# Hybrid trunk on one core: the last output group's weights loaded and split beside the first two output groups

## The chip, the cores and the metric

The kernel runs on one core of a Trainium2 chip. The metric is device time in microseconds (us) of one execution. A core has TensorE (PE, the matmuls), VectorE (DVE), ScalarE (ACT), GpSimd (POOL) and SyncE (SP, which here only issues DMA transfers). Each engine works through its own instructions in program order and waits at an instruction until the results it needs are there.

## The reference

One residual layer over 256 tokens of 2048 channels. A normalised input is projected to all branch inputs; three branches (stick-breaking attention, a Mamba-2 scan and memory cross-attention) run on it; their outputs are projected to 2048 channels, gated and added. The change is in what follows:

```python
merged = (g_sb * (o_sb @ w_branch_sb[layer])
          + g_ssd * (o_ssd @ w_branch_ssd[layer])
          + g_mem * (o_mem @ w_branch_mem[layer]))
x = x + merged @ w_out[layer]
return rms_norm(x, final_norm_w)
```

The output projection `merged @ w_out` is 256 x 2048 by 2048 x 2048 in float32. The final norm needs the squares of all 2048 columns of a token before any column can be scaled.

## The kernel before

A float32 product is made of three products at a faster format: each operand is split into a high part and a low part, and high x high, high x low and low x high are summed in PSUM. `split` (L142 on) does this for weights: ACT copies the raw chunk to the high part `wh` (L146), and DVE subtracts it from the raw chunk to get the low part `wl` (L150).

`gemm` (L249 on) multiplies all 256 tokens by a *group* of 512 output columns. It runs over the 2048 inputs in eight *chunks* of 256. For each chunk, SP loads a 512 KB piece of the weight matrix into a tile `raw` (L207), ACT and DVE split it, and PE runs twelve matmuls of 512 columns (L266 to L268; two rows of 128 inputs, two halves of 128 tokens, three products each). There are four `raw` buffers, three `wh` and three `wl` buffers. A load can be issued when the DVE split that last read its buffer is done; ACT can write a `wh` buffer when PE has finished the chunk three before. The pool gives a new load the buffer that was released first in program order. After each chunk `gemm` calls `pump`, which first runs work that was put off for a number of chunks (`defer`) and then takes one step of one of two lanes of background work, the lanes taking turns. A group's results are read out by an evacuation put off by three chunks, so that it stands behind the third chunk of the next group.

The output projection has four groups. Groups 0 to 2 go through `gemm` (`for g in range(3)`). Their evacuation `out_half` adds the residual on DVE (L885, tile `yo`), squares the sum on ACT (L887, `junk`) and multiplies by the norm weight on POOL (L888). In ACT's queue each group's residual `xr` (512 KB) is loaded when the group's code begins, and ahead of group 0 stand the final norm weights `fw` too (1 MB, L879).

Group 3 is different, so that the first 128 tokens can be normalised and written while PE works on the last 128. All eight of its chunks are loaded and split into their own tiles, `wlh` (high) and `wll` (low), in 8 KB slots of the large pool. Then `drain` runs what was put off. Then PE makes token half 0 as one product of 512 columns, and token half 1 as two products of 256 columns (L954 to L956). `last_cols` reads each product out (L897 to L903) and `write_out` scales and stores (L907 to L917). These three products take their PSUM accumulators from the pool `psA`, which has two buffers in turn and also serves `gemm`. The other pool, `psB`, has four banks and serves the background (the transposes `mt`, for one, L838).

In group 0 there is one piece of other PE work: after its fourth chunk, eight transposes `mt` of the last 512 merged columns, which ACT and DVE split into `mT` two chunks later.

In these words a chunk is named by its group and number, so that g0c4 is the fifth chunk of group 0, and a0 to a7 are the eight chunks of group 3's weights. The order of all loads is the program order of SP: g0c0 ... g2c7, a0 ... a7.

Of the kernel before, what the change touches and what calls it, by code (L numbers as in the profile page):

```python
# [10 lines left out]
F32 = mybir.dt.float32  # L11
F32R = mybir.dt.float32r
# [4 lines left out]
P = 128  # L17
D = 2048
T = 256
NKT = D // P  # L20
GW = 512
KC = 2
# [19 lines left out]
def trunk_kernel(  # L42
# [14 lines left out]
    psA = ctx.enter_context(tc.tile_pool(name="psA", bufs=2, space=bass.MemoryType.PSUM))  # L57
# [4 lines left out]
    def nm(s):  # L62
        cnt[0] += 1
        return f"{s}_{cnt[0]}"

    def slot(shape, dt=F32, n="slot"):
        return big.tile(shape, dt, tag="slot", name=nm(n))
# [19 lines left out]
    def bank(shape, n="bank"):  # L87
        return psB.tile(shape, F32, tag="bank", name=nm(n))
# [53 lines left out]
    def split(*parts):  # L142


        for hi, _, src, scale in parts:
            nc.scalar.activation(hi, src, AF.Copy, **({} if scale is None else {"scale": scale}))  # L146
        for hi, lo, src, scale in parts:
            h32 = hi.bitcast(F32)
            if scale is None:
                nc.vector.tensor_tensor(lo, src, h32, ALU.subtract)  # L150
            else:
                nc.vector.scalar_tensor_tensor(lo, src, scale, h32, ALU.mult, ALU.subtract)
# [15 lines left out]
    lanes = [deque(), deque()]  # L168
# [3 lines left out]
    def defer(fn, chunks=LATE):  # L172

        cnt[0] += 1
        heapq.heappush(late, (now[0] + chunks, cnt[0], fn))
# [22 lines left out]
    def drain():  # L198
        while lanes[0] or lanes[1] or late:
            pump()  # L200
# [4 lines left out]
    def load_chunk(w, c0, width, k0, kc):  # L205
        raw = stage.tile([P, kc, width], F32, tag="raw", name=nm("raw"), bufs=RAWB)
        nc.sync.dma_start(  # L207
            raw, w[k0 * P:(k0 + kc) * P, c0:c0 + width].rearrange("(k p) n -> p k n", p=P))
        return raw
# [39 lines left out]
    def gemm(lhs, nk, w, c0, evac):  # L249

        acc2 = psA.tile([P, 2, GW], F32, tag="acc", name=nm("acc"), bufs=2)
        acc = [acc2[:, 0], acc2[:, 1]]
        kc = KC
        for k0 in range(0, nk, kc):
            raw = load_chunk(w, c0, GW, k0, kc)
            wh = stage.tile([P, kc, GW], F32R, tag="wh", name=nm("wh"))
            wl = stage.tile([P, kc, GW], F32R, tag="wl", name=nm("wl"))
            split((wh, wl, raw, None))
            for j in range(kc):
                kt = k0 + j  # L260
                lh, ll = lhs.at(kt)
                first, last = kt == 0, kt == nk - 1
                for t in range(2):
                    a = acc[t]
                    tt = slice(t * P, (t + 1) * P)
                    nc.tensor.matmul(a, lh[:, tt], wh[:, j], start=first, stop=False)  # L266
                    nc.tensor.matmul(a, lh[:, tt], wl[:, j], start=False, stop=False)  # L267
                    nc.tensor.matmul(a, ll[:, tt], wh[:, j], start=False, stop=last)  # L268
            pump()
        defer(lambda: evac(acc))  # L270
# [168 lines left out]
    for g in range(4):  # L439
        gemm_cols(memT, NKT, w_mem_kv, 2 * g * P, to_split_cols(kT, 2 * g),  # L440
                  acc=None if g else [bank([P, 2, T], "acc") for _ in range(2)])
# [452 lines left out]
    def last_cols(t, cs, acc, xr):  # L894
        for c in range(cs.start, cs.stop, T):
            yc = yo[t][:, 3 * GW + c:3 * GW + c + T]
            nc.vector.tensor_tensor(yc, acc[:, c - cs.start:c - cs.start + T], xr[:, c:c + T],  # L897
                                    ALU.add)
            junk = tq([P, T], "junk")
            q = ssy[:, t, 3 + c // T:4 + c // T]  # L900
            nc.scalar.activation(junk, yc, AF.Square, scale=D ** -0.5, accum_out=q)
            nc.vector.tensor_tensor(msy[:, t:t + 1], q, msy[:, t:t + 1], ALU.add)
            nc.vector.tensor_tensor(yc, yc, fw[:, 3 * GW + c:3 * GW + c + T], ALU.mult)  # L903

    def write_out(t):
        rs = small([P, 1], "frs")
        nc.gpsimd.tensor_tensor(rs, msy[:, t:t + 1], mhalf[:, 0:1], ALU.pow)  # L907
        for c0, c1, eng, dma in ((0, 256, nc.vector, nc.sync), (256, 640, nc.scalar, nc.scalar),
                                 (640, 1152, nc.vector, nc.sync),
                                 (1152, 1536, nc.scalar, nc.scalar),  # L910
                                 (1536, 2048, nc.vector, nc.sync)):
            o = yo[t][:, c0:c1]
            if eng is nc.vector:
                eng.tensor_scalar(o, o, rs, None, ALU.mult)
            else:
                eng.activation(o, o, AF.Copy, scale=rs)
            dma.dma_start(out[t * P:(t + 1) * P, c0:c1], o)  # L917

    def x_chunk(g):
        xr = t4([P, 2, GW], "xr")  # L920
        nc.scalar.dma_start(
            xr, x[:, g * GW:(g + 1) * GW].rearrange("(t p) n -> p t n", p=P))
        return xr

    def out_evac(g):
        xr = x_chunk(g)
        def evac(acc):
            for t in range(2):
                out_half(t, g, acc[t], xr[:, t])
        return evac  # L930

    for g in range(3):
        gemm(mT[0], NKT, w_out, g * GW, out_evac(g))


    g = 3
    xr = x_chunk(g)
    his, los = [], []
    for k0 in range(0, NKT, KC):
        if k0 % 4 == 0:  # L940
            his.append(slot([P, 4, GW], F32R, "wlh"))
            los.append(slot([P, 4, GW], F32R, "wll"))
        raw = load_chunk(w_out, g * GW, GW, k0, KC)
        split((his[-1][:, k0 % 4:k0 % 4 + KC], los[-1][:, k0 % 4:k0 % 4 + KC], raw, None))
    drain()
    for t in range(2):
        tt = slice(t * P, (t + 1) * P)
        for cs in (slice(0, GW),) if t == 0 else (slice(0, T), slice(T, GW)):
            acc = psA.tile([P, 2, GW], F32, tag="acc", name=nm("acc"),
                           bufs=2)[:, 0, 0:cs.stop - cs.start]  # L950
            for kt in range(NKT):
                lh, ll = mT[0].at(kt)
                wh, wl = his[kt // 4][:, kt % 4, cs], los[kt // 4][:, kt % 4, cs]
                nc.tensor.matmul(acc, lh[:, tt], wh, start=(kt == 0), stop=False)  # L954
                nc.tensor.matmul(acc, lh[:, tt], wl, start=False, stop=False)
                nc.tensor.matmul(acc, ll[:, tt], wh, start=False, stop=(kt == NKT - 1))  # L956
            last_cols(t, cs, acc, xr[:, t])
        write_out(t)
# [42 lines left out]
```

## Time and profile before

| | |
|---|---|
| median of three runs | 1228.02 us (1227.74 to 1228.5) |
| the profiled execution's span, first to last instruction | 1226.6 us |
| median less span | 1.4 us |
| PE busy | 1215.5 us (99%) |
| mean granted TensorE clock | 0.998 |
| groups 0 to 2 and group 3 on PE | from about 1128 to 1194.4, and 1194.4 to 1218.5 us |
| from PE's last matmul to the end of the span | about 8 us |

The profile describes one execution. Times of its rows count from the first instruction. In the rows of a timeline the first number is the start, the second the time to the end of the last instruction of the row; brackets give the idle time of the engine before it and what ended it. A row that says SPq or ACTq is the issue of a transfer, not the transfer. Matmuls overlap in the array: a row of 0.39 us does not mean that the next starts 0.39 us later.

### The profile page before, as it was taken

How to read it: one execution, taken by the hardware profiler on the slowest of the kernel's cores; microseconds unless marked ns; L12 is line 12 of the kernel's file. 1: busy time of each engine (PE TensorE's matmuls, PEld its weight loads, DVE VectorE, ACT ScalarE, POOL GpSimd, SP SyncE). 2: the span in 40 equal slices, each digit the busy share in tenths (PEclk: the TensorE clock that was granted, in tenths of full speed). 3: DMA queues.
4: the chain of work that ended last, by engine and by line, in shares of the span. 5: the costliest groups of instructions: out<-in, count | busy, mean ns of one | idle time of the engine just before them, and what ended most of it. 6: DMA issues, size and time to landing. Idle time of an engine off the chain costs nothing.

```text
span 1226.6 us, 16569 instructions
## 1 busy us (share of the span) xinstructions
PE 1215.5 (99%) x6388; PEld 1034.8 (84%) x6388; DVE 784.2 (64%) x990; ACT 649.1 (53%) x875; POOL 51.2 (4%) x50
## 2 busy tenths in 40 slices
PE   9999999999999999999999999999999999999997
PEld 7888888888888888888888888888888888888886
DVE  5686554565654555888888758676777755555554
ACT  6765443554445454545665756475756544444443
POOL 0000000000000000010100000000000010110101
PEclk9999999999999999999999999999999999999999
DMA  9966566655566656565567667686766666567673
GB/s 340 342 197 187 163 194 189 187 168 165 166 180 182 187 172 182 169 182 173 177 185 223 207 200 218 180 231 181 231 184 192 202 195 205 188 197 240 204 240 107
DMA packets 175023, 242.70 MB, mean 198 GB/s; under 512 B 10272, under 2 KB 109792, under 8 KB 174816
## 3 DMA queue, kind: packets, MB, share of 16 engines
q1 hardware_dynamic: 168224, 229.51, 61.2%
q10 hardware_dynamic: 6720, 12.13, 3.0%
q8 instruction: 50, 0.82, 0.3%
q14 instruction: 29, 0.24, 0.1%
HBM read 239.48 MB, written 2.13 MB: 197 GB/s over the span
## 4 chain that ended last, share of the span: by engine, by line
PE 96%; DMA 1%; issue 1%; DVE 1%; ACT 1%; SPq 0%; POOLq 0%; POOL 0%; ACTq 0%
PE acc L229 29%; PE acc L266 15%; PE acc L267 15%; PE acc L268 15%; PE acc L233 14%; PE acc L398 1%; PE acc L399 1%; PE acc L397 1%; PE y L773 1%; DMA raw<-in_w_out_dram 1%; DMA raw<-in_w_mem_kv_dram 1%; PE dtp L459 0%; PE xp L730 0%; PE mt L838 0%; PE spo L649 0%
## 5 line engine op out<-in xcount | busy, mean ns | idle before, releaser
L150 DVE TENSOR_TENSOR wl<-raw,wh 128x1024 fp32r<-128x1024 f32 (+1 forms) x409 | 502.8, 1233 | 310.3 <-ACT wh L146 308.1
L146 ACT ACTIVATE wh<-raw 128x1024 fp32r<-128x1024 f32 (+1 forms) x409 | 431.0, 1055 | 382.5 <-PE acc L268 200.7
L229 PE MATMUL acc<-hT,wh 128*128 128x512 f32 x1408 | 444.0, 397 | 0.0
L233 PEld LDWEIGHTS acc<-hT,wl 128*128 128x128 f32 x1408 | 264.5, 188 | 62.5
L233 PE MATMUL acc<-hT,wl 128*128 128x256 f32 x1408 | 276.8, 278 | 0.0
L229 PEld LDWEIGHTS acc<-hT,wh 128*128 128x128 f32 x1408 | 214.4, 189 | 0.1
L266 PE MATMUL acc<-wh,hT 128*128 128x512 f32 x448 | 175.9, 393 | 0.0
L267 PE MATMUL acc<-wl,hT 128*128 128x512 f32 x448 | 174.7, 390 | 0.0
L268 PE MATMUL acc<-wh,hT 128*128 128x512 f32 x448 | 174.6, 390 | 0.0
L266 PEld LDWEIGHTS acc<-wh,hT 128*128 128x128 f32 x448 | 84.1, 188 | 17.7 <-ACT sq L146 0.5
L268 PEld LDWEIGHTS acc<-wh,hT 128*128 128x128 f32 x448 | 84.1, 188 | 17.8
L267 PEld LDWEIGHTS acc<-wl,hT 128*128 128x128 f32 x448 | 84.1, 188 | 17.4 <-DVE wl L150 0.6
L266 PE MATMUL acc<-wh,oD 128*128 128x512 f32 x128 | 49.8, 389 | 0.0
L267 PE MATMUL acc<-wl,oD 128*128 128x512 f32 x128 | 49.8, 389 | 0.0
L268 PE MATMUL acc<-wh,oD 128*128 128x512 f32 x128 | 49.8, 389 | 0.0
L687 DVE SCALAR_TENSOR_TENSOR cT<-cu,wcols,cT 128x255 f32<-128x255 f32 (+2 forms) x96 | 46.4, 483 | 3.4
L858 POOL TENSOR_TENSOR merged<-merged,sig 128x512 f32<-128x512 f32 x16 | 25.1, 1588 | 521.9 <-DVE sig L857 521.9
L229 PE MATMUL acc<-memT,wh 128*128 128x512 f32 x128 | 40.5, 398 | 0.0
L266 PE MATMUL acc<-wh,mT 128*128 128x512 f32 x96 | 37.4, 390 | 0.0
L268 PE MATMUL acc<-wh,mT 128*128 128x512 f32 x96 | 37.4, 389 | 0.0
L267 PE MATMUL acc<-wl,mT 128*128 128x512 f32 x96 | 37.4, 389 | 0.0
L630 POOL TENSOR_TENSOR lm<-lm,sp 128x384 f32<-128x384 f32 x8 | 13.1, 1639 | 394.7 <-DVE sp L629 385.0
(250 smaller groups left out, 1301.4 us busy)
## 6 DMA issues: line engine op xcount, KB each, us to landing
raw<-in_w_in_dram SPq DMA_DIRECT2D x288, 512.0 KB, 3.8
raw<-in_w_branch_ssd_dram SPq DMA_DIRECT2D x32, 512.0 KB, 4.1
raw<-in_w_out_dram SPq DMA_DIRECT2D x32, 512.0 KB, 5.1
raw<-in_w_mem_kv_dram SPq DMA_DIRECT2D x31, 512.0 KB, 6.6
raw<-in_w_branch_mem_dram SPq DMA_DIRECT2D x16, 512.0 KB, 4.1
raw<-in_w_branch_sb_dram SPq DMA_DIRECT2D x16, 512.0 KB, 4.5
dec<-acT SPq DMA_DIRECT2D x24, 256.0 KB, 6.2
sig<-in_b_gate_dram ACTq DMA_DIRECT2D x12, 256.0 KB, 4.7
```

The source lines that it names most:

```text
L146: nc.scalar.activation(hi, src, AF.Copy, **({} if scale is None else {"scale": scale}))
L150: nc.vector.tensor_tensor(lo, src, h32, ALU.subtract)
L229: nc.tensor.matmul(halves[b], wh[:, kt - k0, b * P:(b + 1) * P], lhs.both(kt), start=first, stop=False, skip_group_check=True)
L233: nc.tensor.matmul(halves[b][:, 1], wl[:, kt - k0, b * P:(b + 1) * P], lhs.at(kt)[0], start=False, stop=last, skip_group_check=True)
L266: nc.tensor.matmul(a, lh[:, tt], wh[:, j], start=first, stop=False)
L267: nc.tensor.matmul(a, lh[:, tt], wl[:, j], start=False, stop=False)
L268: nc.tensor.matmul(a, ll[:, tt], wh[:, j], start=False, stop=last)
L397: nc.tensor.matmul(a, lh[:, tt], wh[:, g], start=first, stop=False)
L398: nc.tensor.matmul(a, lh[:, tt], wl[:, g], start=False, stop=False)
L630: nc.gpsimd.tensor_tensor(lm, lm, sp, ALU.subtract)
L687: nc.vector.scalar_tensor_tensor(a[:, s:T], u[:, 0:T - s], convw[:, 3 - s, i:i + 1], a[:, s:T], ALU.mult, ALU.add)
L858: nc.gpsimd.tensor_tensor(merged[t][:, cs], merged[t][:, cs], sig[:, t], ALU.add)
```

## The change

The loads and splits of a0 to a7 are made a generator, `ahead_steps`, that is put on lane 0 before group 0. Every second `pump` takes a step: it loads one chunk of group 3 through the same four `raw` buffers, and puts its split off by one chunk. So four of the eight chunks go into group 0 and four into group 1. Token half 1's accumulators come from `psB` in place of `psA`. No instruction is added or removed on PE, ACT, DVE, POOL or SP apart from where they stand.

```diff
-    for g in range(3):
-        gemm(mT[0], NKT, w_out, g * GW, out_evac(g))
-
-
-    g = 3
-    xr = x_chunk(g)
     his, los = [], []
-    for k0 in range(0, NKT, KC):
+
+    def ahead(k0):
+
         if k0 % 4 == 0:
             his.append(slot([P, 4, GW], F32R, "wlh"))
             los.append(slot([P, 4, GW], F32R, "wll"))
-        raw = load_chunk(w_out, g * GW, GW, k0, KC)
-        split((his[-1][:, k0 % 4:k0 % 4 + KC], los[-1][:, k0 % 4:k0 % 4 + KC], raw, None))
+        raw = load_chunk(w_out, 3 * GW, GW, k0, KC)
+        ks = slice(k0 % 4, k0 % 4 + KC)
+        hi, lo = his[-1][:, ks], los[-1][:, ks]
+        defer(lambda: split((hi, lo, raw, None)), 1)
+
+    def ahead_steps():
+        for k0 in range(0, NKT, KC):
+            ahead(k0)
+            yield
+
+    lanes[0].append(ahead_steps())
+    for g in range(3):
+        gemm(mT[0], NKT, w_out, g * GW, out_evac(g))
+
+
+    g = 3
+    xr = x_chunk(g)
     drain()
     for t in range(2):
         tt = slice(t * P, (t + 1) * P)
         for cs in (slice(0, GW),) if t == 0 else (slice(0, T), slice(T, GW)):
-            acc = psA.tile([P, 2, GW], F32, tag="acc", name=nm("acc"),
-                           bufs=2)[:, 0, 0:cs.stop - cs.start]
+            if t == 0:
+                acc = psA.tile([P, 2, GW], F32, tag="acc", name=nm("acc"), bufs=2)[:, 0]
+            else:
+                acc = bank([P, T], "acc")
```

On ACT the copies of group 3's weights stood together behind group 2, from the residual's load on (before):

```order
L921 DMA xr_10098<-in_x_dram 128x2x512
L146 ACTIVATE wlh_10100<-raw_10102 128x1024
L146 ACTIVATE wlh_10100<-raw_10106 128x1024
L146 ACTIVATE wlh_10110<-raw_10112 128x1024
L146 ACTIVATE wlh_10110<-raw_10116 128x1024
L146 ACTIVATE wlh_10120<-raw_10122 128x1024
L146 ACTIVATE wlh_10120<-raw_10126 128x1024
```

They now stand between the copies of groups 0 and 1. ACT's rows from the first chunk of group 0 to its seventh, after the change (`wh` are chunks g0c0 to g0c6, `wlh` are a0, a1 and a2, `mT` the split of the transposes):

```order
L146 ACTIVATE wh_9628<-raw_9626 128x1024
L146 ACTIVATE wh_9646<-raw_9644 128x1024
L146 ACTIVATE wh_9668<-raw_9666 128x1024
L146 ACTIVATE wlh_9662<-raw_9664 128x1024
L146 ACTIVATE wh_9692<-raw_9690 128x1024
L146 ACTIVATE wh_9722<-raw_9720 128x1024
L146 ACTIVATE wlh_9662<-raw_9718 128x1024
L146 ACTIVATE wh_9742<-raw_9740 128x1024
L146 ACTIVATE mT_8529<-mt_9708 128x2x256
L146 ACTIVATE mT_8529<-mt_9713 128x2x256
L146 ACTIVATE wh_9768<-raw_9766 128x1024
L146 ACTIVATE wlh_9762<-raw_9764 128x1024
```

The copies of a0, a1 and a2 come one chunk of the group later than their loads: a0 (raw_9664) is loaded ahead of g0c2 (raw_9666) and split behind it. DVE's rows follow the same order.

The loads on SP from the first chunk of group 0, after the change:

```order
L207 DMA raw_9626<-in_w_out_dram 128x2x512
L207 DMA raw_9644<-in_w_out_dram 128x2x512
L207 DMA raw_9664<-in_w_out_dram 128x2x512
L207 DMA raw_9666<-in_w_out_dram 128x2x512
L207 DMA raw_9690<-in_w_out_dram 128x2x512
L207 DMA raw_9718<-in_w_out_dram 128x2x512
L207 DMA raw_9720<-in_w_out_dram 128x2x512
L207 DMA raw_9740<-in_w_out_dram 128x2x512
L207 DMA raw_9764<-in_w_out_dram 128x2x512
L207 DMA raw_9766<-in_w_out_dram 128x2x512
```

In the order of the rows these are g0c0, g0c1, a0, g0c2, g0c3, a1, g0c4, g0c5, a2, g0c6. By the rule of the pool the load of g0c4 waits for the split of g0c2, g0c5 for that of a0, a2 for that of g0c3, and g0c6 for that of g0c4; before, g0c4 waited for g0c0 and g0c6 for g0c2. The even chunks go on so: g1c0 takes the buffer of g0c6, g1c2 that of g1c0, g1c4 that of g1c2, g1c6 that of g1c4 and g2c0 that of g1c6.

The third place is the evacuation of group 0 in group 1, on ACT after the change (`junk` are the two squares; `wh_9853` is g1c2, `wlh_9847` a4, `wh_9881` g1c3):

```order
L146 ACTIVATE wh_9853<-raw_9851 128x1024
L887 ACTIVATE junk_9870,ssy<-yo_9617 128x512
L887 ACTIVATE junk_9874,ssy<-yo_9618 128x512
L146 ACTIVATE wlh_9847<-raw_9849 128x1024
L146 ACTIVATE wh_9881<-raw_9879 128x1024
```

The squares stood between g1c2 and g1c3 before too; a4's copy is new between them and g1c3.

More of the change, by code (lines that the diff above doesn't have):

```diff
@@ L930, in out_evac @@
         return evac
+    his, los = [], []
+    def ahead(k0):
+        if k0 % 4 == 0:
+            his.append(slot([P, 4, GW], F32R, "wlh"))
+            los.append(slot([P, 4, GW], F32R, "wll"))
+        raw = load_chunk(w_out, 3 * GW, GW, k0, KC)
[7 more added lines that the diff above has]
+    lanes[0].append(ahead_steps())
     for g in range(3):
@@ L937, in trunk_kernel @@
     xr = x_chunk(g)
-    his, los = [], []
-    for k0 in range(0, NKT, KC):
-        if k0 % 4 == 0:
-            his.append(slot([P, 4, GW], F32R, "wlh"))
-            los.append(slot([P, 4, GW], F32R, "wll"))
-        raw = load_chunk(w_out, g * GW, GW, k0, KC)
-        split((his[-1][:, k0 % 4:k0 % 4 + KC], los[-1][:, k0 % 4:k0 % 4 + KC], raw, None))
     drain()
```

## The prediction

> **What bounds the kernel now.** I read the page's span and chain first, then the chain of waits in order of time over the last 40 us, where the edited code is.
>
> ```profile
> span 1226.6 us, 16569 instructions
> PE 96%; DMA 1%; issue 1%; DVE 1%; ACT 1%; SPq 0%; POOLq 0%; POOL 0%; ACTq 0%
> ```
>
> PE sets the time nearly everywhere. The 1% of DMA lies at the end:
>
> ```profile
> 1186.41 1.07 ACT wh L146
> 1187.50 1.24 DVE wl L150
> 1188.76 5.97 DMA raw<-in_w_out_dram
> 1194.76 1.07 ACT wlh L146
> 1195.85 1.24 DVE wll L150
> 1197.10 4.94 DMA raw<-in_w_out_dram
> 1202.06 1.07 ACT wlh L146
> 1203.16 1.23 DVE wll L150
> 1204.38 0.61 DVE yo L885
> ...
> 1206.12 0.61 DVE yo L885
> ```
>
> Start and length of each link: two turns of one raw buffer. DVE frees it, a load lands 5 to 6 us later, ACT and DVE split it. Then come group 2's results, which stand behind all those splits on DVE. What this costs PE is in PE's timeline:
>
> ```profile
> 1172.61 0.39 PE L266 MATMUL acc<-wh,mT 128*128 128x512 f32 x1
> 1172.84 0.39 PE L267 MATMUL acc<-wl,mT 128*128 128x512 f32 x1
> ...
> 1194.37 0.39 PE L954 MATMUL acc<-wlh,mT 128*128 128x512 f32 x1
> ...
> 1204.44 0.50 PE L955 MATMUL acc<-wll,mT 128*128 128x512 f32 x1 [0.16 <-DVE wll L150]
> ...
> 1206.77 0.39 PE L954 MATMUL acc<-wlh,mT 128*128 128x256 f32 x1 [0.90 <-DVE yo L885]
> ...
> 1218.26 0.28 PE L956 MATMUL acc<-wlh,mT 128*128 128x256 f32 x1
> ```
>
> Group 2 begins at 1172.61 and ends at 1194.37: 21.76 us for eight chunks, 2.72 us each, 0.2267 us per matmul. The 48 matmuls of token half 0 should take 48 x 0.2267 = 10.88 us, to 1205.25; the next product begins at 1206.77. **So the whole cost of the late weights and of the shared accumulators is 1.52 us**, of which 0.90 is the wait for group 2's readout. Group 1 must then begin at 1150.85 and group 0, with the transposes in it, at about 1128.1:
>
> ```profile
> 1139.24 0.87 PE mt L838 x8
> ```
>
> (1150.85 - 21.76 - 0.87 to 1.0.) How much room is there in groups 0 and 1, where the work goes? First the engines and the DMA by stretch (length; busy time of PE, PEld, DVE, ACT, POOL; PE's clock; DMA share; GB/s):
>
> ```profile
> 1118.00:1129.00 11.00, 11.00 (x50) 9.13 (x49) 4.90 (x4) 4.08 (x5) 0.00 (x0) 1.00 0.86 298
> 1140.00:1185.00 45.00, 45.00 (x201) 37.27 (x200) 25.12 (x23) 21.18 (x27) 5.12 (x4) 1.00 0.64 207
> 1185.00:1200.00 15.00, 15.00 (x68) 12.43 (x67) 9.10 (x8) 8.04 (x8) 0.00 (x0) 1.00 0.82 279
> ```
>
> DVE is busy 25.12 of 45 us and ACT 21.18, so they have time for four more splits a group. DMA is at 0.64. Then the time from issue to landing of the 512 KB loads, in this order: all 32 loads of this matrix; those of 1171.5 to 1181; of 1142 to 1156; of 1119 to 1128.4, when 1.5 MB of norm weights and residual are loaded beside them; of 1186 to 1192, the burst for group 3.
>
> ```profile
> DMA to landing us min/median/max: 3.5/5.1/8.7
> ...
> DMA to landing us min/median/max: 3.5/3.6/3.6
> ...
> DMA to landing us min/median/max: 4.9/5.0/5.9
> ...
> DMA to landing us min/median/max: 5.3/7.5/8.7
> ...
> DMA to landing us min/median/max: 6.0/6.8/7.3
> ```
>
> And how far ahead of PE the splits are (start, length, operation, idle time before):
>
> ```profile
> 1128.68 1.06 ACT L146 ACTIVATE wh<-raw 128x1024 fp32r<-128x1024 f32 x1 [1.94 <-DMA raw<-in_w_out_dram]
> 1153.29 1.28 DVE L885 TENSOR_TENSOR yo<-acc,xr 128x512 f32<-128x512 f32 x2
> 1155.25 1.04 ACT L146 ACTIVATE wh<-raw 128x1024 fp32r<-128x1024 f32 x1
> 1167.37 1.06 ACT L146 ACTIVATE wh<-raw 128x1024 fp32r<-128x1024 f32 x1 [1.66 <-PE acc L268]
> 1168.46 1.23 DVE L150 TENSOR_TENSOR wl<-raw,wh 128x1024 fp32r<-128x1024 f32 x1 [1.49 <-ACT wh L146]
> ```
>
> The last two rows are the split of group 2's first chunk. It is done at 1169.69, and the first matmul that reads the low part is at 1172.84: **3.1 us of slack**. ACT cannot run further ahead, since it waits for PE to free a high-part buffer.
>
> **The change part by part.**
>
> *The tail.* With group 3's weights split long before, the 0.16 wait and its slow restart go. Token half 1 takes background banks, last used by the transposes around 1140, so the 0.90 wait goes too. Gain: 1.52 us, and no more: everything behind (the two 256-column products, 1206.77 to 1218.26, and the chain from there to the end) has the same instructions. What is late next in the tail is the readout of group 2, which now stands ahead of nothing that PE waits for.
>
> *ACT and DVE in groups 0 and 1.* Eight pairs move there, 4 x (1.06 + 1.23) us a group. By busy time they cost nothing. Two details matter below: order, and the buffers that they hold.
>
> *The loads.* In two chunks of PE's work, 5.44 us, SP must now get three loads through four buffers. By the order of SP's rows each even chunk of a group takes the buffer of the even chunk before. So one turn of a buffer must fit into 5.44 us: the load's landing time L, ACT's copy, DVE's subtraction, the next issue. The chain above has the last three: copy begins 1194.76, next load 1197.10, 2.34 us. A turn is L + 2.34. **It fits only where L is below 3.1 us, and no load of the 32 landed in under 3.5.** Before, a buffer had four chunks, 10.88 us, for its turn, and L could be 8.5. What hid L was that time, and the change halves it for the even chunks.
>
> There are seven such turns: g0c2 to g0c4, on to g0c6, g1c0, g1c2, g1c4, g1c6 and g2c0. Behind g2c0 nothing more is loaded ahead. Each turn makes PE late by L - 3.1, once the slack is used up. How much slack is there at the start? Before, the third chunk of group 0 was already late (the row at 1128.68, a wait for its load). In the new order a0 has that place in the queue and g0c2 comes one behind, issued 2.72 us later into the same congestion, so it lands near 1131; its split ends near 1133.3. PE wants its low part at 1128.1 + 5.44 + 0.23 = 1133.8. That leaves 0.5 us, and the transposes in group 0 give 1.0 more: 1.5 us.
>
> L cannot be read directly, since the trace of before never has three loads in 5.44 us for long. From below: 3.5, the fastest. From above: 6.0, the fastest of the burst. An even chunk's load goes out first of three, when the earlier ones have mostly landed, which speaks for the lower half; but the DMA share rises to about 0.96 (0.64 x 1.5), which speaks against 3.5. I take 4.35, half way between 3.6 and the median 5.1. A turn is then 6.69 us, 1.25 too long: 7 x 1.25 = 8.75, less 1.5 of slack, 7.25 us. At L = 3.5 it is 2.8 - 1.5 = 1.3; at 5.1, 14.0 - 1.5 = 12.5; at 6.0, 20.3 - 1.5 = 18.8.
>
> *The readout of group 0.* In group 1 the two squares hold ACT from DVE's readout at 1153.29 to 1155.25, 1.96 us, and then g1c3 is split. The slack hid this. Now a4's copy (1.06) stands between, and where chunks come just in time the readout begins as PE reaches the second matmul of g1c2. The low part of g1c3 is ready 1.96 + 1.06 + 1.06 + 1.23 = 5.3 us after that; PE wants it after 2.72. Cost 2.6 us once. While PE waits the ring catches up, so one turn's excess comes off: 2.6 - 1.25 = 1.35 us net. Bounds: nothing if some slack is left, 2.6 if none of it is given back.
>
> *The sum.* -1.52 + 7.25 + 1.35 = +7.1 us. The execution of 1226.6 becomes 1233.7. The median lies 1.4 above the span (1228.02), so the forecast is 1235.1 us, slower by 0.6%.
>
> **The rivals.**
>
> *The loads keep up.* For: DMA has a share of 0.36 free, and the loads of 1171.5 to 1181 landed in 3.6. If all do so, a turn is 0.4 to 0.5 too long; with 1.5 to 3.1 us of slack the seven turns cost 0 to 2, and the readout stays hidden by what is left. Net -1.5 to +0.5: 1226.5 to 1228.5, not slower. It decides at L of about 3.5. Against: the four loads of 1142 to 1156 took 4.9 to 5.9 with only one load per chunk. 20%.
>
> *The DMA engines become the bound.* A group now needs 8 + 4 weight loads and a residual, 13 x 0.524 MB in 21.76 us, 313 GB/s. The stretch of 1118 to 1129 reached 298 at loads of 5.3 to 8.7 us, the burst 279 at 6.0 to 7.3. If L settles at 6.0, +18.8 - 1.5 = +17.3: 1245; at 6.8, 7 x 3.7 - 3.0 = +23: 1251. Against: PE's own lateness lowers the demand, so the queue can't stay full. 12%.
>
> *PE's clock falls.* At the end of the span, after PE's last matmul at 1218.26:
>
> ```profile
> 1218.40:1222.40 4.00, 0.14 (x2) 0.00 (x0) 2.06 (x6) 1.74 (x4) 0.68 (x1) 1.00 0.16 57
> 1222.40:1226.40 4.00, 0.00 (x0) 0.00 (x0) 0.00 (x0) 0.00 (x0) 0.00 (x0) 0.50 0.56 205
> ```
>
> The granted clock halves about 4 us after PE goes idle. A single stall of 4 us (a turn with L above 7.1) would then be followed by chunks at half speed, 2.72 us lost on each until it recovers; with two or three such stalls, some 10 to 15 us beyond the stalls: 1255 or more. My stalls are 1 to 3 us, so 3%. [...]
>
> *More than the tail.* A gain of over 2.5 us needs something beyond the 1.52 that PE's rows leave. I find no place for it: 3%, at about 1225.
>
> That the change doesn't do what it says can be left out: the rows of the order show a0 to a7 between the chunks of groups 0 and 1.
>
> **How the numbers follow.** The forecast case (even chunks late, L between 3.5 and 5.1, 1230 to 1240) has 62%; keeping up 20%, DMA-bound 12%, the clock 3%, a gain 3%. Predicted 1235.1. The range for 8 in 10: 1227 to 1244; it takes in most of the first rival and the near end of the second, and leaves out the clock, the far end and the gain. Within 0.2%, about what a measurement of this kernel can tell from no change (1225.6 to 1230.5), lie the first rival and the lowest edge of the forecast: 23%. Faster 3%, slower 74%.
>
> **What would show it.** In the changed profile: PE waiting for `wl` of L150, and ACT for `raw` from `w_out`, in groups 0 and 1, by 8 to 11 us in all, where both are close to nothing now; PE's group 0 to group 2 taking 9 us more than 1128.1 to 1194.37; SP waiting for DVE right before the even chunks' loads; landing times of 4 to 5 us there. The tail step is right if token half 0's 48 matmuls take 10.9 us and the next product follows without a gap. The forecast is wrong if the even chunks' loads land in 3.5 us or less, or if PE shows no wait in groups 0 and 1: then the time is 1226.5 and I have misjudged the slack.

## The result, and the profile after

The changed kernel takes 1242.82 us, the median of four runs (1241.82 to 1245.8), beside 1228.08 us (1227.74 to 1228.5) for the kernel before on the same chip. The ratio is 1.0124, with a 95% interval of 1.011 to 1.0139: slower by 14.7 us, where 7.1 was forecast. The execution profiled, which took 1245.8, is the slowest of the four, so its span is up to 3 us longer than that of the median.

Span and chain by engine:

```profile
span 1243.8 us, 16568 instructions
PE 92%; DMA 4%; ACT 1%; DVE 1%; issue 1%; POOLq 0%; POOL 0%; ACTq 0%
```

DMA is now 4% of the chain; it was 1%. The chain of waits in order of time over groups 0 to 2 (start, length, what):

```profile
1122.73 7.92 DMA raw<-in_w_out_dram
...
1133.10 4.37 DMA raw<-in_w_out_dram
1137.57 1.07 ACT wh L146
1138.66 1.24 DVE wl L150
1139.91 6.07 DMA raw<-in_w_out_dram
...
1148.41 5.78 DMA raw<-in_w_out_dram
...
1156.64 4.01 DMA raw<-in_w_out_dram
...
1163.10 4.94 DMA raw<-in_w_out_dram
...
1170.48 6.89 DMA raw<-in_w_out_dram
...
1179.82 6.42 DMA raw<-in_w_out_dram
...
1188.72 0.79 PE acc L267
```

From 1120.38 to 1188.72 the chain has no matmul in it. The first load shown is g0c2's; its split ends at 1133.10, where the prediction had 1133.3. The other seven, 55.6 us from the first issue to the last split, are those of g0c4, g0c6, g1c0, g1c2, g1c4, g1c6 and g2c0, each issued as the split of the one before ends. PE runs beside this ring of one buffer and waits for it (start, length, operation; in brackets the wait). The rows start with the waits of g2c0, whose low part PE multiplied at 1172.84 before:

```profile
1187.46 0.50 PE L266 MATMUL acc<-wh,mT 128*128 128x512 f32 x1 [2.06 <-ACT wh L146]
1188.72 0.79 PE L267 MATMUL acc<-wl,mT 128*128 128x512 f32 x1 [0.76 <-DVE wl L150]
1189.31 0.63 PE L268 MATMUL acc<-wh,mT 128*128 128x512 f32 x1
...
1194.43 0.51 PE L268 MATMUL acc<-wh,mT 128*128 128x512 f32 x1
...
1213.16 0.39 PE L967 MATMUL acc<-wlh,mT 128*128 128x512 f32 x1
...
1224.05 0.28 PE L967 MATMUL acc<-wlh,mT 128*128 128x256 f32 x1
```

From these rows the 17.2 us between the spans (1243.8 less 1226.6) are put together:

- up to the first matmul on g2c0's low part: 1188.72 - 1172.84 = **15.9 us late**;
- from there to the start of group 3: 24.44 us (to 1213.16) where it was 21.53 (1172.84 to 1194.37): **2.9 us**. Between 1189.31 and 1194.43 matmuls start 0.43 us apart, not 0.227;
- from there to the end: 30.64 us (1213.16 to 1243.8) where it was 32.23: **-1.6 us**, the gain at the tail. Token half 0 takes 10.89 us and the next product follows without a wait.

The second item is PE's clock. By stretch (length; busy time of PE, PEld, DVE, ACT, POOL; PE's granted clock; DMA share; GB/s):

```profile
1150.00:1160.00 10.00, 7.78 (x28) 5.72 (x27) 4.15 (x4) 2.96 (x3) 0.00 (x0) 0.86 0.66 232
1160.00:1170.00 10.00, 7.66 (x32) 5.80 (x31) 6.40 (x6) 6.15 (x9) 2.54 (x2) 0.97 0.51 168
1170.00:1180.00 10.00, 9.58 (x36) 7.39 (x35) 4.25 (x5) 3.73 (x5) 0.00 (x0) 0.83 0.77 252
1180.00:1190.00 10.00, 7.18 (x27) 5.37 (x28) 4.63 (x5) 4.08 (x5) 0.00 (x0) 0.89 0.60 210
1190.00:1200.00 10.00, 10.00 (x35) 7.99 (x35) 6.59 (x6) 3.78 (x8) 2.54 (x2) 0.77 0.75 257
```

The clock falls three times, at the waits of 1.46 + 0.76, 0.51 + 1.84 and 2.06 + 0.76 us. DMA's share is 0.51 to 0.77, over the five stretches no higher than before (0.66 in the mean, 0.68 before): the DMA engines are idle a third of the time while PE waits for loads. What each engine waits for between 1110 and 1244 (us in total, times, longest) names the same place; before, this line was 1.9 us, once:

```profile
ACT wh L146 <- DMA raw<-in_w_out_dram: 33.1, 9, 5.9
```

### The profile page after: what moved, and what is told of

Its sections match the earlier page's. It is cut to its first block, busy times and chain, and to the rows that moved or that the text cites. A ratio compares the mean times of both kernels' runs of the same rounds, so it can differ in the third digit from the quotient of the medians.

```text
span 1243.8 us, 16568 instructions
## 1 busy us (share of the span) xinstructions
PE 1224.1 (98%) x6388; PEld 1039.9 (84%) x6388; DVE 784.2 (63%) x990; ACT 647.5 (52%) x875; POOL 52.3 (4%) x50
## 4 chain that ended last, share of the span: by engine, by line
PE 92%; DMA 4%; ACT 1%; DVE 1%; issue 1%; POOLq 0%; POOL 0%; ACTq 0%
PE acc L229 29%; PE acc L233 14%; PE acc L266 13%; PE acc L267 13%; PE acc L268 13%; DMA raw<-in_w_out_dram 4%; PE acc L397 1%; PE acc L398 1%; PE acc L399 1%; PE y L773 1%; DVE wl L150 1%; ACT wh L146 1%; DMA raw<-in_w_mem_kv_dram 0%; PE dtp L459 0%; PE acc L969 0%
## 5 line engine op out<-in xcount | busy, mean ns | idle before, releaser
L267 PE MATMUL acc<-wl,mT 128*128 128x512 f32 x96 | 40.6, 423 | 6.0 <-DVE wl L150 6.0
L266 PE MATMUL acc<-wh,mT 128*128 128x512 f32 x96 | 40.0, 417 | 4.0 <-ACT wh L146 4.0
L268 PE MATMUL acc<-wh,mT 128*128 128x512 f32 x96 | 39.8, 415 | 0.0
```

## The experiments

The theory after the result: the change loses because a load ahead shortens the turn of a `raw` buffer from four chunks to two, and a load's landing, copy, subtraction and next issue don't fit. The rivals: the added bytes slow all loads; the added splits, by their place in ACT's and DVE's queues, delay the others; the clock.

### The banks alone

The kernel before, with only the accumulators of token half 1 moved:

```diff
+            if t == 0:
+                acc = psA.tile([P, 2, GW], F32, tag="acc", name=nm("acc"), bufs=2)[:, 0]
+            else:
+                acc = bank([P, T], "acc")
```

> One part alone: only token half 1's accumulators are moved to the background's banks; the weights of group 3 are loaded and split at the end as before. Theory (the tail is 1.52 us, 0.90 of it the wait for group 2's readout, the rest the late eighth chunk): the wait of 0.90 us and its restart go, the 0.16 wait for wll stays; 1226.9 to 1227.2 us, 0.9 to 1.2 under before. Rival (the wait only moves to the next thing that is late, DVE's readout in the tail): within 0.3 us of before.

Measured: 1227.12 us (1226.8 to 1229.92) beside 1228.1; ratio 0.9994 (0.9985 to 1.0003). The span is 1225.2, 1.4 shorter, and token half 1 begins 11.23 us after token half 0 in place of 12.40. This half of the change does what it was costed at, and the median alone can't tell it from nothing.

### Buffers of their own

The whole change, but the loads ahead land, in halves, in tiles that are idle there:

```diff
-        raw = load_chunk(w_out, 3 * GW, GW, k0, KC)
+        for j in range(KC):
+            r = (ta if k0 // KC % 2 else tb)([P, GW], "raw_ahead")
+            nc.sync.dma_start(r, w_out[(k0 + j) * P:(k0 + j + 1) * P, 3 * GW:4 * GW])
```

> The change, but the loads ahead land in buffers of their own (eight tiles of 256 KB that are idle at the end), so that the four raw buffers serve groups 0 to 2 alone, as before. The bytes are the same and are loaded in the same places; the loads ahead are 16 of 256 KB in place of 8 of 512 KB. Theory 'buffers' (the even chunks' turn through a raw buffer is too long): the turn is four chunks again, 10.88 us, against landing times of up to 7 us plus 2.34, so PE does not wait in groups 0 and 1, the clock stays at 1.00, and the tail's gain is left: 1226.5 to 1227.5 us. Rival 'DMA' (12 loads and a residual in a group's time are more than the DMA engines bring): landing times stay at 6 us and more, PE waits by 5 to 10 us: 1232 to 1240 us.

Measured: 1228.08 us beside 1228.1; ratio 0.9999 (0.999 to 1.0009). The loss is gone, with the same bytes, and the same splits (in halves) in the same queues. Its stretches, with the columns as above:

```profile
1140.00:1150.00 10.00, 10.00 (x50) 8.34 (x49) 7.79 (x10) 6.50 (x10) 0.00 (x0) 1.00 0.99 336
1150.00:1160.00 10.00, 10.00 (x46) 8.29 (x45) 6.89 (x8) 6.45 (x11) 2.99 (x2) 1.00 0.87 313
```

PE is busy all of the time at the full clock while DMA stands at 0.99 and 336 GB/s. In the change the DMA engines moved 168 to 257 GB/s and PE waited. The loads through the four `raw` buffers are no faster than in the change: those issued from 1139 to 1155 landed in 5.8 to 6.8 us. So neither the bytes nor the DMA engines bound it; the time that a buffer has for its turn did.

The gain of about 1 us that was expected isn't in the median. In the profiled execution the tail's part is there (token half 0 takes 10.88 us, and the next product follows without a wait), but groups 0 to 2 take 0.45 us more, and group 0 begins 1.41 us later (1129.61, before 1128.20). Of that, 0.8 us are there 100 us into the program already, long before the edited code. Why it begins later, and whether it does so in every execution, isn't shown.

### The buffer held without a load

The load ahead replaced by a write of one column into a tile of the same ring:

```diff
+        raw = stage.tile([P, KC, GW], F32, tag="raw", name=nm("raw"), bufs=RAWB)
+        defer(lambda: nc.vector.memset(raw[:, 0, 0:1], 0.0), 1)
```

> Buffers without bytes: at the places of the loads ahead a raw buffer is taken and given back one chunk later by a one-column write, but nothing is loaded or split; group 3's weights come at the end as before, token half 1 lies in the background's banks. Theory 'buffers': even chunks wait for the even chunk before, turn L + 2.34 with L of 3.6 to 4.9 at the lighter traffic: PE waits 3 to 9 us in groups 0 and 1, 1230 to 1236 us. Rival 'DMA': without the added bytes nothing is late, 1227 us as with the banks alone.

Measured: 1227.29 us; ratio 0.9993. The expectation failed because this wasn't the test meant. The buffers went round in another order than in the change: the shortest turn was three chunks (8.16 us), and PE had no wait in groups 0 to 2 with loads that landed in 3.7 to 6.3 us (those issued from 1132 to 1184). It tells only that a turn of three chunks is enough for such loads, and led to the next experiment on it.

### The buffer held by a load of 8 KB

The ring goes round exactly as in the change, but the loads ahead bring 8 KB, and group 3 is loaded and split at its old place:

```diff
+        raw = stage.tile([P, KC, GW], F32, tag="raw", name=nm("raw"), bufs=RAWB)
+        nc.sync.dma_start(raw[:, 0, 0:16], w_out[k0 * P:(k0 + 1) * P, 3 * GW:3 * GW + 16])
+        defer(lambda: nc.vector.tensor_copy(raw[:, 0, 16:32], raw[:, 0, 0:16]), 1)
```

> Buffers without bytes, mended: at the place of each load ahead a raw buffer is taken by an 8 KB load (1/64 of the bytes) and given back one chunk later, behind a 16-column copy on DVE. The buffers pass from load to load exactly as in the change (each even chunk takes the buffer of the even chunk before). Nothing of group 3 is split early; its weights come at the end as before, token half 1 lies in the background's banks. Theory 'turn' (an even chunk's turn, L + 2.34, must fit into 5.44 us whatever fills the other buffers): with L of 3.8 to 5 at the lighter traffic each of seven turns is 0.7 to 1.9 us too long, less 1.8 of slack: PE is 3 to 11 us late, 1230 to 1238 us. Rival 'bytes' (it needs the added bytes): 1227 to 1228 us, as with the banks alone.

Measured: 1240.67 us (1240.41 to 1240.98) beside 1228.33; ratio 1.0099 (1.0084 to 1.0114). Of the 14.7 us, 12.3 are there without the bytes and without the early splits. This run still has its late group 3, so it lacks some of the tail's gain. Its chain of waits:

```profile
1132.76 4.58 DMA raw<-in_w_out_dram
...
1139.80 4.11 DMA raw<-in_w_out_dram
...
1146.34 6.94 DMA raw<-in_w_out_dram
...
1155.72 3.94 DMA raw<-in_w_out_dram
...
1168.31 4.60 DMA raw<-in_w_out_dram
...
1175.36 6.38 DMA raw<-in_w_out_dram
```

The loads still take 3.9 to 6.9 us. Between the fourth and the fifth the chain goes through group 0's readout (L885, L887). The rival "bytes" falls; the upper end of what the theory expected was still 2.7 us too low.

### Half the bytes of every load

The change with every instruction and buffer in its place, but with loads of `w_out` half the size, so that the product is another one:

```diff
+        if w is w_out:
+            nc.sync.dma_start(raw[:, 0], w[k0 * P:(k0 + 1) * P, c0:c0 + width])
+            return raw[:, 0:1].to_broadcast([P, kc, width])
```

> The change with every instruction and every buffer as it is, but each load of the output projection brings only the first half of its chunk (256 KB), and both rows of the split read that half, so that the product is another one. Theory (a turn of a buffer is the landing time plus 2.34 us against 5.44 us, and the change loses by the landing time of 512 KB, 5.5 us in the mean of the even chunks): half the bytes should land in 3 to 4 us, so a turn takes 5.3 to 6.3 us and the seven turns are at most 0 to 4 us late; with what the readouts cost where the slack is used up, 1227 to 1234 us, and even chunks that land in under 4.2 us. Rival (the order of the splits on ACT and DVE, with group 3's between the others', costs it, whatever the loads take): 1238 to 1243 us.

Measured: 1232.2 us (1231.62 to 1232.62) beside 1227.91; ratio 1.0033 (1.002 to 1.0045). The loads' median from issue to landing is 3.5 us, against 6.1 in the change (issues between 1130 and 1195; the last column). The change first, this run second:

```profile
raw<-in_w_out_dram SPq DMA_DIRECT2D x25, 512.0 KB, 6.1
```

```profile
raw<-in_w_out_dram SPq DMA_DIRECT2D x26, 256.0 KB, 3.5
```

With that, 10.4 of the 14.7 us are gone. Two even chunks took longer than expected (g1c0 4.89 us, g1c6 4.58). What stays is one place, the readout of group 0 (chain of waits):

```profile
1155.81 0.70 DVE yo L888
1156.53 1.34 ACT junk L890 x4
1157.87 0.96 ACT wlh L146
...
1160.86 1.22 DVE wl L150
```

The squares, then a4's copy, then g1c3's split: the readout term of the prediction. In PE's timeline it costs 0.96 + 1.81 us:

```profile
1159.81 0.50 PE L269 MATMUL acc<-wh,mT 128*128 128x512 f32 x1 [0.96 <-ACT wh L146]
1162.13 0.50 PE L270 MATMUL acc<-wl,mT 128*128 128x512 f32 x1 [1.81 <-DVE wl L150]
...
1163.16 0.60 PE L271 MATMUL acc<-wh,mT 128*128 128x512 f32 x1
...
1166.54 0.43 PE L270 MATMUL acc<-wl,mT 128*128 128x512 f32 x1
```

And behind the two waits the granted clock falls (0.90 in the mean from 1160 to 1164, 0.68 from 1164 to 1168), and eight matmuls start 0.42 us apart: 3.38 us (1163.16 to 1166.54), 1.6 more than 8 x 0.2267. So the three come to 2.8 + 1.6 - 1.6 (tail) = 2.8; the spans differ by 3.0 (1229.6 against 1226.6).

### Split right behind the load

The splits of group 3 are no longer put off by a chunk; the turn of a buffer becomes 2.67 chunks, 7.25 us:

```diff
-        defer(lambda: split((hi, lo, raw, None)), 1)
+        split((hi, lo, raw, None))
```

> The change, but each chunk loaded ahead is split right behind its load in program order, not one chunk later. The bytes and the places of the loads are the same; the order in which buffers come free is now the order of the loads, so that a buffer's turn is four loads, 2.67 chunks or 7.25 us on average, in place of two chunks for the even ones. Theory 'turn': 7.25 us fits L up to 4.9; with L near 5.5 a turn is 0.6 too long, six turns, less 1.8 of slack: 1227 to 1231 us. Rival 'bytes' (12 loads and a residual in 21.76 us are too many for DMA with this ring, in whatever order the buffers pass): 1238 to 1243 us.

Measured: 1235.65 us (1234.96 to 1237.38); ratio 1.0061 (1.0046 to 1.0076). Half of the loss is gone, less than was expected. Four of the loads in its chain took 5.6 to 6.3 us, and their turns 7.6 to 8.6. Two of PE's waits (1.62 and 1.49 us) follow a readout.

### A load ahead after every fourth chunk, and the same two chunks later

A second `yield` behind each step puts six of the eight loads beside groups 0 to 2 and makes every turn three chunks, 8.16 us:

```diff
             ahead(k0)
             yield
+            yield
```

> The change with a load ahead after every fourth chunk in place of every second: six of the eight chunks of group 3 are loaded in groups 0 to 2, the last two at the end. The buffers then pass over three chunks each, 8.16 us. Theory 'turn': L + 2.34 fits for all L up to 5.8, so PE waits by 0 to 2 us in all: 1226.5 to 1229 us. Rival 'each load ahead through the ring has its price' (six of eight loads, six eighths of the 14.7 us): 1236 to 1239 us.

Measured: 1236.97 us (1235.81 to 1238.31); ratio 1.0073 (1.0056 to 1.009). The theory missed by 8 us, and the rival's number was right. But PE's waits are three, not six, and all alike:

```profile
1138.91 0.50 PE L267 MATMUL acc<-wl,mT 128*128 128x512 f32 x1 [1.96 <-DVE wl L150]
...
1163.93 0.50 PE L267 MATMUL acc<-wl,mT 128*128 128x512 f32 x1 [1.84 <-DVE wl L150]
...
1189.79 0.51 PE L267 MATMUL acc<-wl,mT 128*128 128x512 f32 x1 [1.83 <-DVE wl L150]
```

A readout stands behind the third chunk of each group (in group 0 that of the last branch, L857), and every second of these splits of group 3 comes right behind it. ACT's and DVE's rows ahead of the second wait:

```profile
1157.59 1.28 DVE L885 TENSOR_TENSOR yo<-acc,xr 128x512 f32<-128x512 f32 x2
...
1158.93 0.62 ACT L887 ACTIVATE junk<-yo 128x512 f32<-128x512 f32 x1
...
1159.55 1.05 ACT L146 ACTIVATE wlh<-raw 128x1024 fp32r<-128x1024 f32 x1
1160.50 2.93 ACT L146 ACTIVATE wh<-raw 128x1024 fp32r<-128x1024 f32 x3
```

If this is so, the same loads two chunks later, away from the readouts, should cost nothing. One more `yield` ahead of the loop does that:

```diff
     def ahead_steps():
+        yield
         for k0 in range(0, NKT, KC):
```

> The same sparse loads ahead as in the run with every fourth chunk (six of eight beside groups 0 to 2, every turn of a buffer three chunks, 8.16 us), but each load and its split two chunks later, so that no split of group 3 stands right behind a readout in ACT's queue. Theory (what was left in that run, three waits of PE of 1.8 to 2.0 us, is a split of group 3 standing between a readout and the next chunk's split): at most one wait of PE of over 1 us in groups 0 to 2, and 1227 to 1230 us. Rival (each load ahead costs by itself, about 1.4 us for each of the six, wherever it stands): 1235 to 1239 us, with as many waits as there.

Measured: 1227.3 us (1226.58 to 1227.63) beside 1228.33; ratio 0.9991 (0.9982 to 1.0). PE has no wait left in groups 0 to 2, and ACT's line of waits for loads (1120 to 1230) is down to this:

```profile
ACT wh L146 <- DMA raw<-in_w_out_dram: 13.6, 8, 2.6
```

Its span is 1224.6, 2.0 less than the kernel before. The same loads, the same ring, the same number of splits: 9.7 us lie between the medians only by where they stand. The loads are hardly faster: those issued from 1133 to 1188 landed in 3.6 to 6.8 us in the first run, in this one in 3.7 to 6.5 (from 1131 to 1187). In the profiles groups 0 to 2 take 74.90 us in the first and 66.17 in this one, 8.7 of the 9.3 us between the spans. Of these the three waits are 5.6, a stretch at half clock behind the second (0.67 in the mean from 1164 to 1168) 1.6, and the rest the slower matmuls right before and behind the waits. One thing isn't separated: the first load ahead also moves out of the time in which the norm weights and the residual are loaded (there it took 8.8 us), which bears on the first wait.

### Filling PE's waits

Two kernels add matmuls that nobody reads, to keep PE busy: five ahead of each of twelve chunks in the first, nine ahead of g2c0 alone in the second.

> The change with five matmuls that nobody reads (1.13 us at full clock) ahead of each of the twelve chunks from the sixth of group 0 to the first of group 2, to fill PE's waits with work. Theory 'clock' (of the 18.6 us that groups 0 to 2 take longer in the changed profile, about 6 are matmuls at half clock after waits of 2 to 3 us): the clock stays at 1.00 and the time falls by 4 to 7 us to 1236 to 1239 us, although 13.6 us of PE work are added. Rival 'waits alone' (PE follows the loads, whatever its clock): the end of group 2 is set by the loads, and the time stays at 1242 to 1244, or goes up to 1250 where the filling comes on top.

> The change with nine matmuls that nobody reads (2.0 us at full clock) ahead of group 2's first chunk only, where the last wait of the ring stands (2.06 us and 0.76 us, followed by some 13 matmuls at half clock). Theory 'the clock costs only behind the last turn': PE stays busy in that wait, the clock stays at 1.00, and the 13 matmuls take 0.2 us less each: 2.0 to 2.9 us under the change, 1240.0 to 1240.8 us. Rival 'the clock is not on the path': 1242.5 to 1243.5 us, or above where the filling comes on top.

Measured: 1244.59 and 1243.69 us, both no better than the change's 1242.82. The first was a poor test: 60 more matmuls are 13.6 us of work, and behind 1139.4 its chain of waits runs through PE, so PE itself was the bound. In the second the granted clock at that place did stay at full speed (1.00 from 1180 to 1200):

```profile
1187.33 2.20 PE L263 MATMUL idle<-mT 128*128 128x512 f32 x9
...
1190.46 0.51 PE L274 MATMUL acc<-wl,mT 128*128 128x512 f32 x1 [0.69 <-DVE wl L150]
```

From 1190.46 to the end of its span (1243.0) are 52.5 us, against 55.1 (1188.72 to 1243.8) in the change: 2.6 us less behind the wait. From g0c4's load to g2c0's low part it took the same 55.6 us, though its chain goes through group 0's readout on the way; it began later, at 1134.86 and not at 1133.10, of which 1.26 us lie ahead of group 0. So the profiles put the clock's price there at 2.6 us, while the medians show no gain; what part of the 14.7 us it is in the median run stays open.

### Buffers of their own, from the end of group 0 on

As in the run with buffers of their own, with three steps let pass first:

```diff
+        for _ in range(3):
+            yield
         for k0 in range(0, NKT, KC):
```

> Buffers of their own for the loads ahead, as in the earlier run with them, but beginning at the end of group 0, when the burst of norm weights and residual is over. Theory (with the four raw buffers left to groups 0 to 2, the whole gain of 1.5 us at the tail remains): 1226.4 to 1227.2 us and no wait of PE of over 0.5 us between the first chunk of group 0 and the end of group 3. Rival (the splits ahead take from the slack of groups 1 and 2 what the tail gains): 1228 to 1230 us.

Measured: 1229.36 us (1228.27 to 1229.93) beside 1228.33; ratio 1.0005 (0.9997 to 1.0014). No gain: it fits the rival more than the theory. PE waits 0.32 and 0.59 us behind the readouts of groups 0 and 1, where copies of group 3 stand next to the squares again, and in all groups 0 to 2 take 67.68 us, 1.5 more than before. The tail's gain is there (10.89 us for token half 0). Another 1.0 us lies ahead of group 0 in the profiled execution, which begins at 1129.20.

The fastest are thus the banks alone (1227.12) and the sparse loads placed between the readouts (1227.3), each about 1 us under the kernel before, with intervals that reach 1.0. Since the second has the moved banks too, the medians show no gain of loading ahead.

## Why the prediction was half right

*The tail: right.* Forecast -1.52 us; measured -1.6, no wait, 10.89 us for the 48 matmuls.

*The ring: the mechanism right, its size wrong.* Seven turns from g0c4's load to g2c0's split, each issue at the end of the split before, ACT waiting for `raw`, PE for `wl`: all in the rows. The step that failed is "I take 4.35" for L. The seven loads took 4.37, 6.07, 5.78, 4.01, 4.94, 6.89 and 6.42 us, 5.5 in the mean, above 5.1, the upper end of the forecast case. The forecast's own sum with 5.5 gives 7 x 2.4 - 1.5 = 15.3, and 15.9 was measured; seven turns are 38.5 us of landing and 17.1 of the rest, 2.45 each where 2.34 was read.

The reason given for the lower half holds for three of the seven: "an even chunk's load goes out first of three, when the earlier ones have mostly landed". Where nothing had been issued in the 3 us ahead (g0c4, g1c2, g1c4), the load took 4.37, 4.01 and 4.94 us, 4.44 in the mean and close to 4.35. The other four had 512 KB loads issued 1.0 to 2.3 us ahead of them and took 5.78 to 6.89. At g0c6 that was a2 (1138.47), at g1c6 both g1c5 and a6 (1168.15, 1169.29), since three splits on DVE ended there within 2.4 us (from 1168.1 to 1170.5) and freed their buffers close together. At g1c0 and g2c0 it was the residual of the group, on ACT's queue:

```profile
1147.41 0.38 ACTq L921 DMA_DIRECT2D xr<-in_x_dram  x1
...
1178.77 0.37 ACTq L921 DMA_DIRECT2D xr<-in_x_dram  x1
```

The run with loads of 8 KB has its two longest ring loads at the same place (6.94 and 6.38 us, issued 0.9 and 1.0 us behind a residual). The profile before could have told: the load issued at 1143.04, next to a residual, is the one of 5.9 in the row "4.9/5.0/5.9" (five loads, not four).

```profile
1142.95 0.44 ACTq L921 DMA_DIRECT2D xr<-in_x_dram  x1
...
DMA to landing us min/median/max: 5.9/5.9/5.9
```

So L was neither the steady stretch's 3.6 nor the burst's 6.8, but a mix by what had been issued just ahead. That the neighbours set it is read from these rows; no run takes a residual away. With half the bytes the ring's waits were gone.

*The readout of group 0: the size right, its place in the sum wrong.* The gross 2.6 us was measured as 2.8 with half loads, where nothing else is late. In the change itself it lies beside the ring and adds nothing to the 15.9: the chain has no L885 in it, and where the chain goes through the readout (the second kernel with filled waits) the 55.6 us are the same. I added 1.35 for it. And it is not only group 0's: wherever a split of group 3 stands behind a readout and the slack is used up, 1.8 to 2.0 us go, as in the run with every fourth chunk.

*The rivals.* "The loads keep up" fell: no ring load of 3.5 us. "The DMA engines become the bound" came nearer with its time (1245, for loads of 6.0 us) but had the wrong cause: the share stayed at 0.51 to 0.77, and with more buffers 336 GB/s hurt nobody. "The clock falls" was given 3% because its edge was read from one idle stretch at the end of the program. It fell at waits of 2.2 to 2.8 us in all. That was the second thing missing from the sum: 2.9 us behind g2c0 in the profiled execution. The earlier two slow stretches lie beside the ring: the chain has no matmul there.

*The waits.* Forecast: PE waits 8 to 11 us in groups 0 and 1. It waits 10.0, in groups 0 to 2, yet the groups lose 18.6 (1128.35 to 1213.16 is 84.8 us, before 66.2). Of the other 8.6, some 5.7 are matmuls that start at half clock (0.50, 0.43 us apart); the rest lies in the matmuls right before and behind the nine waits, which overlap less (0.34 us to the next start behind a wait, not 0.227). Waits alone understate a loss.

## What to carry to other kernels

Before work is put into "free" time, count the turns of every buffer that it takes: a ring is paid at the landing time that a load has with others issued just ahead of it (here 5.8 to 6.9 us), on SP's queue or on ACT's, and not at that of a load alone (4.0 to 4.9). In the change late splits came close together, and the loads with them: the three on DVE ahead of g1c6's load ended within 2.4 us, and it took 6.89. An added step on an engine with slack belongs away from the other occasional steps there; the same six loads and splits cost 9 us with every second split behind a readout, and nothing two chunks on. Here a DMA share of 0.66 with an engine waiting for loads meant too few buffers, not too few bytes per second.

## What the runs showed of the hardware

PE's granted clock halved behind much shorter waits than the 4 us that I read at the end of the program: 1.46 + 0.76, 0.51 + 1.84 and 2.06 us in the change. There it stands at 0.50 from 1157.1 to 1160.5, from 1170.8 to 1174.2 and from 1187.8 to 1194.7 us. That is for 3.4, 3.4 and 6.8 us. Three stretches of the change, right ahead of the first fall, in it, and one with no fall behind it (columns as above):

```profile
1153.70:1157.10 3.40, 1.18 (x5) 0.57 (x4) 1.72 (x2) 2.81 (x3) 0.00 (x0) 1.00 0.39 151
1157.20:1160.40 3.20, 3.20 (x9) 2.41 (x9) 1.68 (x2) 0.05 (x1) 0.00 (x0) 0.50 0.65 209
...
1136.65:1140.05 3.40, 1.80 (x9) 1.30 (x8) 3.18 (x3) 2.09 (x3) 0.71 (x1) 1.00 0.54 180
```

In the 3.4 us ahead of the first fall PE is busy 1.18 us and idle 2.22; ahead of the other two it is idle for 1.84 and 2.06 us. In the last stretch shown it is idle 1.60, and the clock stays at 1.00 behind it.

The length of a wait alone doesn't tell whether the clock falls. In the run with every fourth chunk it fell behind the wait of 1.84 us (0.67 in the mean from 1164 to 1168); behind those of 1.96 and 1.83 us it stayed at 1.00. With nine filling matmuls ahead of g2c0 it stayed at 1.00 from 1170 to 1200, a wait of 1.84 us included. With the split right behind the load, where PE waits 1.62 us, it stood at 1.00 from 1130 to 1200. What decides between such waits isn't shown.
